# Layer 0's opening of a two-layer transformer on one core: first norm, modulation, keys, values and gates in a hand-written order

## The chip, the core and the metric

The kernel runs on one core of a Trainium2 chip. Its engines work in parallel, each in its own program order: TensorE (PE) multiplies matrices, VectorE (DVE), ScalarE (ACT) and GpSimd (POOL) do elementwise work, and SyncE (SP) issues the DMAs between HBM and SBUF. They meet through semaphores; an instruction that waits holds back everything behind it on its own engine. The metric is the device time of one execution in microseconds (us), lower is better. Before the change the median of three runs is 2780.57 us (2779.29 to 2788.6).

## The reference, cut to what matters

Two layers; the change touches only the beginning of layer 0: the modulated norm of 256 context and 1024 latent tokens, the projection to keys and values of the windowed attention, the 16 gates of the mLSTM, and the first queries.

```
mod_l = (silu(c) @ ada_w[0] + ada_b[0]).reshape(b, 1, 6, 1024)      # mod_c the same from c_ctx
h = rms_norm(x, norm1_g[0]) * (1 + mod[:, :, 1]) + mod[:, :, 0]     # for latents and for context
qa, ka, va, oa, ga, qb, kb, vb = split(h @ w_in)                    # 4 x 512, 16, 512, 128, 128 columns
g = (ga + gate_b) -> input gates and log_sigmoid(forget gates), forwards and backwards
qb, kb = rms_norm(qb, q_norm_g), rms_norm(kb, k_norm_g)             # per head of 64, then rope for latents
o_b = banded window attention(qb, kb, vb, context keys and values, sink)
h_a = mLSTM over chunks of 128, both directions (qa, ka, va, g)
y = concat(rms_norm(h_a) * sigmoid(oa), o_b) @ w_out;  x = x + mod[2] * y;  then the MLP;  then layer 1
```

## The kernel before, in words

Activations lie transposed: eight chunks of 128 channels (index j) on the partitions, tokens along the free axis. Tokens come in three groups, `TGS`: L1 (tokens 256 to 767) and L2 (768 to 1279) are latents, 512 columns each, and C (0 to 255) is the context. To multiply nearly in fp32 at the fast rate, each operand is split into a rounded part and a rest (`hhi`/`hlo` of the activations, `whi`/`wlo` of the weights), and each product takes three matmuls. A "unit" is one block of 128 output columns of a weight: 8 chunks x 3 matmuls for each group.

Layer 0 opens in `first` (in `body`). Modulation of shift and scale is made in four quarters (`ada_quarter`, L239): quarter q gives channels of chunks 2q and 2q+1 and needs 2 MB of `ada_w`, in four tiles s0f to s5f in rotation; eight 32-column matmuls (L254) on `cs`, the additions L259 and L261, four small matmuls with `asel2` (L264), and two DVE instructions that write `mod` and `gs`. The norm's sum of squares is taken by `norm_stats` (ACT squares, DVE and POOL add, one matmul with `ones`, L306) for L1 and L2, and by `sum_steps` for C. `norm_apply` makes, for each chunk, x * gs * rs on DVE (L375), `hhi` on ACT (L379), and `hlo` on DVE (L393) for even chunks or on ACT and POOL (L381, L390) for odd ones. The loop at the end of `first` multiplies each ready chunk with two units, the gates' (`U_G`, 16 columns in use out of 128) and the keys' (`U_KB`) at L2381.

Then `swa_setup` projects the values (weights in `mr` and `ir`, L423 to L425), transposes them (L1382), norms the keys (`qk_norm`), and `mixer0` makes the first queries, seven of the 48 steps of `gather` (the mLSTM's units, one group each) and `gates`. `swa` follows: 40 blocks of scores (first matmul L1457), softmax and values, with the remaining units, queries and modulation as fill between the blocks. `mlstm` comes behind it and needs what `gates` makes.

All this is written in Tile: a scheduler orders the instructions of each engine by its own estimates, and a tile's buffer is reused only when its last reader is done. Region reuse (`Area.place`, `Banks`) is by hand.

Of the kernel before, what the change touches and what calls it, by code (L numbers as in the profile page):

```python
# [19 lines left out]
P = 128  # L20
# [23 lines left out]
U_KB, U_VB, U_QB, U_G, U_M = 1, 2, 3, 0, 7  # L44
# [52 lines left out]
class Kernel:  # L97
# [141 lines left out]
    def ada_quarter(self, q, tp, psp):  # L239
# [4 lines left out]
        for kk in range(2):  # L244
            ps = psp.tile("D", "adaps")
            for e in range(2):
                w = tp.tile([P, 2, 2, 256], F32, tag="raw")
                k0 = 4 * kk + 2 * e
                src = a["ada_w"][0, k0 * P : (k0 + 2) * P, 0:2048].rearrange("(k p) (b n) -> p k b n", p=P, b=2)
                for b in range(2):  # L250
                    nc.sync.dma_start(w[:, :, b, :], src[:, :, b, q * 256 : q * 256 + 256])
                for i in range(2):
                    c = 2 * e + i
                    nc.tensor.matmul(  # L254
                        ps[32 * c : 32 * c + 32, :], self.cs[:, k0 + i, :], w[:, i, :, :].rearrange("p b n -> p (b n)"),
                        start=True, stop=True, tile_position=(0, 32 * c),
                    )
            if kk == 0:
                nc.scalar.activation(acc, ps, AF.Copy)  # L259
            else:  # L260
                nc.vector.tensor_tensor(acc, ps, acc, op=ALU.add)  # L261
        pt = psp.tile("D", "adapt")
# [13 lines left out]
        )  # L276

# [211 lines left out]
    def qk_norm(self, ps, t0, n, vv, tabs, g, hd, qscale, tp, ss):  # L489
# [5 lines left out]
        rs = self.qk_rms(n, st, hd, qscale, tp, ss)  # L495
# [698 lines left out]
    def gates(self, kp, cbt, psp, dr, gy):  # L1194

        nc = self.nc
        ta, tb = self.slot(2, F32), self.slot(3, F32R)
# [6 lines left out]
        for x in (mr, ir):  # L1204
            nc.gpsimd.memset(x.bitcast(F32), 0.0)
# [4 lines left out]
        gd = dr.tile([4, 4, T], F32, tag="gd", name="gd")  # L1210
        for i in range(4):
            nc.sync.dma_start(gd[i], gy[32 * i : 32 * i + 4, :])
# [82 lines left out]
    def mixer0(self, first):  # L1295
# [8 lines left out]
        with ExitStack() as ctx:  # L1304
            kp = self.pool(ctx, "kp", side="right")
            with ExitStack() as c2:
# [3 lines left out]
                gy, heads = first(wp, kp)  # L1310
                psp = self.banks(A=(0, 1), B=(2, 3), Q=(4,), S=(5,))
                tp = self.area(6 * PG, 8 * PG)
                self.qt_bufs = 1
                tr = tp.tile([P, 512], F32, tag="qsw")[:, : 2 * P].rearrange("p (d q) -> p d q", d=2)
                nc.sync.dma_start(tr, a["tri"].rearrange("d p q -> p d q"))
                nc.vector.tensor_copy(tri, tr)
# [11 lines left out]
                tb = self.area(5 * PG, 6 * PG)  # L1328
                psa = self.banks(A=(0, 1, 2), B=(7,), Q=(4,), G=(3, 5))
                st, qs = self.swa_setup(sp, tp, tb, psa, wp, heads, gy)  # L1330
                for _ in st[-1](psa, 0, qs):
                    pass
                self.gps = self.banks(A=(6, 7))
                heads = [self.gather(wp, tb, ud, h) for h in range(4)]
                for _ in range(7):
                    next(heads[0])
                mr, ir, cb, tq = self.gates(kp, small, psa, dr, gy)
                self.gps = psp
                self.swa(sp, small, tb, psp, wp, mixd, heads, st, qs)
# [22 lines left out]
    def swa_setup(self, sp, tp, tb, psp, wp, heads, gy):  # L1362

        nc, a = self.nc, self.a
        KH = [sp.tile([P, T], F32R, tag=f"s{v}", name=f"KH{v}") for v in range(2)]
        KL = [sp.tile([P, T], F32R, tag=f"s{2 + v}", name=f"KL{v}") for v in range(2)]
        VV = [sp.tile([P, NT // 2, 2, P], F32R, tag=f"s{4 + i}", name=f"VV{i}") for i in range(2)]
        tt = self.area(0, 2 * PG)
        tabs = self.rope_tables(tt, a["rope0"], V_SK, V_SKS, "r0")
        wp.place("raw", cuts(self.F, PG, 2 * PG))  # L1370
        wp.place("adaraw", cuts(self.F, PG, 3 * PG, 4 * PG))
        tb.tile([P, 512], F32, tag="ev")
        for t0, n, vv in TGS:
            s = slice(t0, t0 + n)
            ps, ks = heads[t0]
            nc.scalar.activation(gy[:, s], ps[:, :n], AF.Identity, bias=self.v(V_GB))
            ps = self.proj(psp, "A", heads["v"], t0, n)
            t = tb.tile([P, 512], F32, tag="adaacc", name="vt")
            nc.scalar.activation(t[:, :n], ps[:, :n], AF.Copy)
            pt = psp.tile("B", "vT")  # L1380
            for i in range(n // P):
                nc.tensor.transpose(pt[:, i * P : (i + 1) * P], t[:, i * P : (i + 1) * P], self.ident)  # L1382
            src = pt[:, :n].rearrange("p (c v d) -> p c v d", v=2, d=64)
            for i in range(2):
                c0, c1 = max(t0 // P, 5 * i), min((t0 + n) // P, 5 * i + 5)
                if c0 < c1:
                    for v in range(2):
                        o = VV[i][:, c0 - 5 * i : c1 - 5 * i, v, :]
                        self.split(o[:, :, 0:64], o[:, :, 64:128], src[:, c0 - t0 // P : c1 - t0 // P, v, :], nc.vector)
            t = self.qk_norm(ks, t0, n, vv, tabs, V_SK, 64, False, tp, psp.tile("Q"))  # L1390
# [8 lines left out]
        tabs = self.rope_tables(tt, a["rope0"], V_SQ, V_SQS, "r0")  # L1399

        def queries(psp, pr, qs):
            w = self.unit(wp, a["win0"][U_QB + pr])
            qs += [self.slot(2 * (pr % 2) + h, F32R) for h in range(2)]
            for t0, n, vv in TGS:
                ps = self.proj(psp, "A", w, t0, n)
                t = self.qk_norm(ps, t0, n, vv, tabs, V_SQ, 64, True, tp, psp.tile("Q"))
                s = slice(t0, t0 + n)
                for h in range(2):
                    src = t[64 * h : 64 * h + 64, :n]
                    own = qs[h][64 * h : 64 * h + 64, s]  # L1410
                    nc.scalar.activation(own, src, AF.Copy)
                    nc.gpsimd.tensor_tensor(
# [1016 lines left out]
```

## Time and profile before

| | |
|---|---|
| median of 3 runs | 2780.57 us |
| the profiled execution | 2788.63 us, its span 2786.8 us |
| PE busy in the span | 2695.9 us (97%) |
| DVE, ACT, POOL busy | 1885.0, 1476.7, 1095.2 us |
| mean granted clock of TensorE | 0.992 |

The page says that PE is the busiest engine at 97%; in its 40 slices only the first shows 6 of 10. A slice is 70 us long, so the opening has to be cut finer. Times in the rows are us from the span's start. Matmul records overlap their neighbours, so the pace of matmuls is read from the distance of their starts, not from their durations.

### The profile page before, as it was taken

Reading aid. Unit: us, or ns where it says so; the run is one execution under the profiler, and the core shown is the slowest. Engines: PE = TensorE matmul, PEld = TensorE weight load, DVE = VectorE, ACT = ScalarE, POOL = GpSimd, SP = SyncE. Lnnn points to the kernel's source line nnn. Section 1 sums busy time; section 2 is a strip of 40 time slices with the busy share of each in tenths; the row PEclk is TensorE's granted clock in tenths of the full one; section 3 lists DMA queues with packets and bytes.
Section 4 is the critical chain, followed back from the end, with each engine's and each line's share of the span. In section 5 each row is a group of like instructions: output and inputs, shape, how many; then the busy total and the mean of one; then the engine's idle time right before and its main releaser. Section 6 shows DMA issues by size and latency. Waiting matters only on the chain.

```text
span 2786.8 us, 40782 instructions
## 1 busy us (share of the span) xinstructions
PE 2695.9 (97%) x14683; PEld 2284.5 (82%) x14683; DVE 1885.0 (68%) x3268; ACT 1476.7 (53%) x2611; POOL 1095.2 (39%) x744
## 2 busy tenths in 40 slices
PE   6899999999999999999999999999999999999999
PEld 3688788878788888878878889999988888888877
DVE  4645655677876766557678757888874677666676
ACT  4654554445564444344436557888865554444432
POOL 3430220000237576530001346787865499740000
PEclk9999999999999999999999999999999999999999
DMA  7122233363335667488756710000045155577664
GB/s 241 56 84 100 79 104 112 108 210 99 110 108 174 209 220 237 157 307 286 246 166 218 243 61 26 24 28 20 26 150 195 65 174 192 175 284 263 215 223 154
DMA packets 194659, 428.33 MB, mean 154 GB/s; under 512 B 21128, under 2 KB 47336, under 8 KB 194456
## 3 DMA queue, kind: packets, MB, share of 16 engines
q1 hardware_dynamic: 194456, 425.73, 45.6%
q8 instruction: 115, 1.88, 0.3%
q14 instruction: 88, 0.72, 0.1%
HBM read 322.90 MB, written 102.74 MB: 153 GB/s over the span
## 4 chain that ended last, share of the span: by engine, by line
PE 73%; DVE 6%; DMA 4%; issue 3%; ACT 2%; POOL 1%; DVEq 0%; SPq 0%; POOLq 0%; ACTq 0%
PE psum L588 21%; PE psum L1046 17%; PE psum L423 4%; PE psum L2017 4%; PE psum L424 4%; PE psum L425 4%; PE psum L2203 3%; PE psum L1142 3%; PE psum L1924 3%; DMA hhiraw<-in_w 2%; DVE W L398 2%; POOL W L398 1%; PE psum L1500 1%; PE psum L2079 1%; PE psum L1506 1%
## 5 line engine op out<-in xcount | busy, mean ns | idle before, releaser
L398 POOL TENSOR_TENSOR W<-F,W 128x512 fp32r<-128x512 f32 (+2 forms) x319 | 489.1, 1547 | 519.4 <-ACT W L397 438.8
L1046 PE MATMUL psum<-W,W 128*128 128x512 f32 x2688 | 617.8, 391 | 10.9 <-DVE W L398 4.7
L1046 PEld LDWEIGHTS psum<-W,W 128*128 128x128 f32 x2688 | 504.6, 188 | 123.6 <-DVE W L398 10.9
L588 PE MATMUL psum<-hhi,W 128*128 128x512 f32 (+1 forms) x1600 | 442.2, 356 | 2.3 <-DVE x L1774 0.9
L397 ACT ACTIVATE W<-F 128x512 fp32r<-128x512 f32 (+2 forms) x380 | 275.1, 739 | 292.6 <-POOL F L561 99.4
L588 PEld LDWEIGHTS psum<-hhi,W 128*128 128x128 f32 x1600 | 285.1, 189 | 46.3 <-issue 2.5
L588 PE MATMUL psum<-hlo,W 128*128 128x512 f32 (+1 forms) x800 | 284.3, 355 | 0.0
L397 ACT ACTIVATE W<-hhiraw 128x1024 fp32r<-128x1024 f32 x98 | 104.0, 1061 | 316.2 <-PE psum L1046 235.4
L423 PE MATMUL psum<-hhi,W 128*128 128x512 f32 (+1 forms) x624 | 232.8, 373 | 0.9 <-ACT F L1432 0.9
L424 PE MATMUL psum<-hlo,W 128*128 128x512 f32 (+1 forms) x624 | 227.3, 364 | 0.0
L425 PE MATMUL psum<-hhi,W 128*128 128x512 f32 (+1 forms) x624 | 227.1, 364 | 0.0
L969 DVE TENSOR_TENSOR hhiraw<-hhiraw 128x512 f32<-128x512 f32 x154 | 108.3, 712 | 108.4 <-DMA hhiraw<-in_w 107.6
L561 POOL TENSOR_TENSOR F<-F 128x512 f32<-128x512 f32 x112 | 164.8, 1471 | 13.5 <-DMA F<-in_w 4.5
L588 PEld LDWEIGHTS psum<-hlo,W 128*128 128x128 f32 x800 | 151.2, 189 | 21.4 <-issue 0.2
L390 POOL TENSOR_TENSOR hlo<-F,hhi 128x512 fp32r<-128x512 f32 (+1 forms) x24 | 27.4, 1144 | 347.6 <-ACT F L381 347.6
L398 DVE TENSOR_TENSOR W<-hhiraw,W 128x1024 fp32r<-128x1024 f32 x98 | 119.6, 1221 | 60.7 <-ACT W L397 58.2
L423 PEld LDWEIGHTS psum<-hhi,W 128*128 128x128 f32 x624 | 118.4, 190 | 21.3 <-ACT x L397 2.5
L424 PEld LDWEIGHTS psum<-hlo,W 128*128 128x128 f32 x624 | 118.5, 190 | 17.3 <-issue 2.2
L425 PEld LDWEIGHTS psum<-hhi,W 128*128 128x128 f32 x624 | 118.3, 190 | 17.3 <-issue 0.5
L588 PE MATMUL psum<-x,W 128*128 128x512 f32 x504 | 123.5, 389 | 0.0
L398 DVE TENSOR_TENSOR W<-hloraw,W 128x1024 fp32r<-128x1024 f32 x98 | 119.4, 1218 | 0.7 <-ACT W L397 0.7
L2203 PE MATMUL psum<-W,W 128*128 128x512 f32 (+1 forms) x408 | 109.5, 372 | 2.4 <-POOL W L398 1.5
(450 smaller groups left out, 6231.2 us busy)
## 6 DMA issues: line engine op xcount, KB each, us to landing
F<-in_w SPq DMA_DIRECT2D x104, 512.0 KB
hloraw<-hd SPq DMA_DIRECT2D x90, 512.0 KB
hhiraw<-in_w SPq DMA_DIRECT2D x72, 512.0 KB
hd<-F SPq DMA_DIRECT2D x142, 256.0 KB
hhiraw<-in_w SPq DMA_DIRECT2D x116, 256.0 KB
F<-in_ada_w SPq DMA_DIRECT2D x96, 256.0 KB
hd<-x SPq DMA_DIRECT2D x90, 256.0 KB
F<-in_win SPq DMA_DIRECT2D x33, 512.0 KB
```

Source lines behind the costliest of these rows:

```text
L397: nc.scalar.activation(hi, src, AF.Copy)
L398: eng.tensor_tensor(lo, src, hi.bitcast(F32), op=ALU.subtract)
L423: nc.tensor.matmul(ps, sh, mh, start=i == 0, stop=False)
L424: nc.tensor.matmul(ps, sh, ml, start=False, stop=False)
L425: nc.tensor.matmul(ps, sl, mh, start=False, stop=i == n - 1)
L561: add = lambda o, p, q, how: nc.gpsimd.tensor_tensor(o, p, q, op=how)
L588: nc.tensor.matmul(ps, w[i][:, p], B[j][k], start=first and j == 0 and m == 0, stop=last and j == 3 and m == 2)
L969: tt = lambda o, p, q, how: eng.tensor_tensor(o, p, q, op=how)
L1046: nc.tensor.matmul(bank(base + i), A[u][:, p], B[v], start=first and m == 0, stop=last and m == 2)
L1142: nc.tensor.matmul(bank(k), B[u][:, i * P : i * P + P], A[v][:, half], start=f == 0 and m == 0, stop=f == NFF - 1 and m == 2,)
L2017: nc.tensor.matmul(u.o[:, :QT], v[x], p[y], start=c == 0 and m == 0, stop=c == 2 * NB - 1 and m == 2)
L2203: self.nc.tensor.matmul(ps, x[:, c], y, start=first and m == 0, stop=last and m == 2)
```

## The change: what it does

1. The opening is issued inside `manual_schedule`: on all engines the instructions stand in the order in which the code issues them, from the first load to the first queries and seven gather steps.
2. Group C is loaded first, then quarter 0, then the units of values and keys, L1, quarter 1, L2, quarters 2 and 3. `ada_quarter` becomes a generator with five steps (load, load, products, products, sums), so loads stand far ahead of the products.
3. Squares are summed by matmuls with `ones` (8 for C, 8 for L1, 4 for L2 after pairwise additions on DVE), not on DVE and POOL.
4. x is scaled by the norm in place for several chunks ahead (`scale`); when a quarter is there, `prepare` makes `hhi` on ACT and the rest on DVE, and POOL has no share in it.
5. Beside keys, the opening multiplies values and not gates. The gates' weight shrinks to 32 columns and is not split: `gate_rows` multiplies it in plain fp32 with `hhi` and `hlo`, the three groups at three column positions, after three gather steps.
6. The first mLSTM unit (`own`) takes the place in `mr` and `ir` that the values' had, and its steps stand between the steps of the key norm.
7. The elementwise part of the gates (`gates`) runs in the last of the four head pairs of `swa`, at its first block.

```diff
+        w0 = load(0)
+        yield
+        w1 = load(1)
+        yield
+        products(0, w0)
+        yield
+        products(1, w1)
+        yield
         pt = psp.tile("D", "adapt")
         for i in range(4):
             nc.tensor.matmul(pt[:, 2 * i : 2 * i + 2], acc[:, i * P : (i + 1) * P], self.asel2, start=True, stop=True)
...
+        def add_up(g, s, j, last=ND - 1):
...
+            nc.tensor.matmul(parts[g], k.ones, s, start=j == 0, stop=j == last)
...
+        def scale(g, js):
...
+            for j in js:
+                nc.vector.tensor_tensor(y, y, rs[g][:, :n], op=ALU.mult)
...
+        def prepare(g, j):
...
+            nc.scalar.activation(hi, y, AF.Identity, scale=gs, bias=sh)
+            if j % 2 and not vv:
+                nc.scalar.activation(h, y, AF.Identity, scale=gs, bias=sh)
+            else:
+                nc.vector.tensor_scalar(h, y, gs, sh, op0=ALU.mult, op1=ALU.add)
+            nc.vector.tensor_tensor(lo, h, hi.bitcast(F32), op=ALU.subtract)
...
+        both(C, 2, 3)
+        scale(L1, range(2, 4))
+        add_up(L2, two_squares(0), 0, 3)
+        both(L1, 2)
...
+        add_up(L2, two_squares(3), 3, 3)
+        rms(L2)
+        run(2)
+        run(3)
...
+        scale(L2, range(4))
+        both(L2, 0, 1)
+        run(2)
+        both(L2, 2)
+        run(2)
+        both(L2, 3)
+        scale(L2, range(4, 6))
+        both(C, 4)
+        both(L1, 4)
+        run(3)
+        both(L2, 4)
...
+        def gate_rows():
+            for j in range(ND):
+                for m, h in enumerate((self.hhi, self.hlo)):
+                    for q, t0, n, o in ps:
+                        nc.tensor.matmul(
+                            o, w[:, j, :], h[:, j, t0 : t0 + n].bitcast(F32),
+                            start=j == 0 and m == 0, stop=j == ND - 1 and m == 1, tile_position=(0, 32 * q),
+                        )
...
+                if (pr, blk) == (3, 0):
+                    g = gates()
```

SP issues the opening's loads. Before (x_118 is chunk 0 of x, s0f to s5f the tiles of a quarter, F the raw weights):

```order
L131 DMA x_125<-in_x 128x512
L414 DMA F<-in_win 128x1024 x3
L251 DMA s0f<-in_ada_w 128x2x256 x2
L251 DMA s1f<-in_ada_w 128x2x256 x2
L251 DMA s2f<-in_ada_w 128x2x256 x2
L251 DMA s3f<-in_ada_w 128x2x256 x2
L131 DMA x_118<-in_x 128x512
```

and now, with the eight loads of C ahead of it:

```order
L131 DMA x_125<-in_x 128x256
L252 DMA s0f<-in_ada_w 128x2x256 x2
L252 DMA s1f<-in_ada_w 128x2x256 x2
L252 DMA s2f<-in_ada_w 128x2x256 x2
L252 DMA s3f<-in_ada_w 128x2x256 x2
L2487 DMA F<-in_win 128x1024 x2
L131 DMA x_118<-in_x 128x512
```

Half as much of x stands ahead of quarter 0, and the three weight loads have become two behind it.

On DVE, quarter 2 read before (L261 adds a quarter's halves, L268 and L273 write `mod` and `gs`, L375 and L393 are `norm_apply`; x_118 to x_125 are chunks 0 to 7 of x):

```order
L261 TENSOR_TENSOR F<-psum,F 128x512
L268 TENSOR_TENSOR mod_82<-psum,vec 128x2x4
L273 SCALAR_TENSOR_TENSOR gs_169<-mod_82,vec 128x4
L375 SCALAR_TENSOR_TENSOR F<-x_122,gs_169,F 128x512
L375 SCALAR_TENSOR_TENSOR F<-x_123,gs_169,F 128x512
L375 SCALAR_TENSOR_TENSOR F<-x_122,gs_169,F 128x512
L393 SCALAR_TENSOR_TENSOR hlo<-F,mod_82,hhi 128x512
```

and the stretch around quarter 2 now (L2516 scales x, L2528 and L2529 are `prepare`, L268 adds the halves, L284 and L289 write `mod` and `gs`):

```order
L2516 TENSOR_TENSOR x_121<-x_121,F 128x512
L2528 TENSOR_SCALAR F<-x_118,gs_172,mod_82 128x512
L2529 TENSOR_TENSOR hlo<-F,hhi 128x512 x2
L268 TENSOR_TENSOR F<-psum,F 128x512
L2528 TENSOR_SCALAR F<-x_120,gs_172,mod_82 128x512
L2529 TENSOR_TENSOR hlo<-F,hhi 128x512
L284 TENSOR_TENSOR mod_82<-psum,vec 128x2x4
L289 SCALAR_TENSOR_TENSOR gs_172<-mod_82,vec 128x4
L2529 TENSOR_TENSOR hlo<-F,hhi 128x512
L2516 TENSOR_TENSOR x_122<-x_122,F 128x512
```

Each addition of a quarter now has `prepare` steps of other chunks behind it.

On PE, quarters 2 and 3 met before as follows (L254 are a quarter's products, L264 its small matmuls, L2381 a chunk's products with W_105, the gates', and W_106, the keys'):

```order
L254 MATMUL psum<-s4f,cs 32x512 x2
L254 MATMUL psum<-s5f,cs 32x512 x2
L264 MATMUL psum<-asel_64,F 128x2 x4
L254 MATMUL psum<-s0f,cs 32x512 x2
L254 MATMUL psum<-s1f,cs 32x512 x2
L2381 MATMUL psum<-hhi,W_105 128x512
L2381 MATMUL psum<-hhi,W_106 128x512
```

and the stretch around quarter 2 now (L2504 sums squares, L261 are a quarter's products, L2539 the chunks' products with W_105, now the values', and W_106, the keys'):

```order
L2504 MATMUL psum<-F,ones 128x512 x2
L261 MATMUL psum<-s2f,cs 32x512 x2
L261 MATMUL psum<-s3f,cs 32x512 x2
L2539 MATMUL psum<-hhi,W_105 128x512 x2
L2539 MATMUL psum<-hlo,W_105 128x512
L2539 MATMUL psum<-hhi,W_106 128x512 x2
L2539 MATMUL psum<-hlo,W_106 128x512
```

A quarter's products come in two separate halves, with the products of one or two chunks between.

## Rows read from the trace of the kernel before

**Rows 1.** Stretches: length, busy of PE, PEld, DVE, ACT, POOL (instructions), clock, DMA, GB/s

```profile
0.00:15.00 15.00, 0.01 (x1) 0.01 (x1) 7.64 (x44) 7.74 (x12) 3.44 (x8) 1.00 0.82 278
15.00:27.00 12.00, 7.96 (x26) 2.24 (x26) 2.43 (x5) 5.43 (x8) 8.04 (x4) 0.98 1.07 366
27.00:40.00 13.00, 10.15 (x31) 4.72 (x32) 6.96 (x10) 7.44 (x14) 2.56 (x2) 0.76 0.91 284
40.00:72.00 32.00, 26.67 (x116) 16.84 (x115) 14.64 (x28) 11.72 (x20) 7.05 (x5) 0.88 0.45 141
72.00:92.38 20.38, 19.38 (x92) 15.50 (x93) 12.62 (x27) 15.46 (x33) 7.76 (x9) 0.86 0.12 31
92.38:166.30 73.92, 64.47 (x321) 51.93 (x320) 32.45 (x55) 39.28 (x75) 33.70 (x22) 1.00 0.23 79
166.30:558.00 391.70, 385.94 (x2319) 320.59 (x2318) 226.99 (x775) 205.51 (x467) 64.35 (x39) 0.99 0.29 98
```

**Rows 2.** Waits of PE in the first 300 us: total, times, longest

```profile
PE psum L306 <- DVE F L321: 15.0, 1, 15.0
PE psum L2381 <- ACT hhi L379: 7.2, 5, 2.1
```

**Rows 3.** Waits of DVE from 15 to 92 us

```profile
DVE F L261 <- PE psum L254: 18.9, 3, 8.7
```

**Rows 4.** PE's timeline, 22 to 62 us: start, length, [idle before it]

```profile
22.20 1.05 PE L254 MATMUL psum<-s3f,cs 128*32 128x512 f32 x4 [0.45 <-DMA s3f<-in_ada_w]
24.10 1.05 PE L264 MATMUL psum<-asel,F 128*128 128x2 f32 x8 [0.85 <-DVE F L261]
27.15 1.22 PE L2381 MATMUL psum<-hhi,W 128*128 128x512 f32 x2 [2.00 <-ACT hhi L379]
...
53.43 0.62 PE L254 MATMUL psum<-s2f,cs 128*32 128x512 f32 x1
53.43 0.62 PE L254 MATMUL psum<-s3f,cs 128*32 128x512 f32 x2
53.45 0.62 PE L254 MATMUL psum<-s4f,cs 128*32 128x512 f32 x1
```

**Rows 5.** PE's timeline, 72 to 95 us, and the first scores

```profile
72.31 1.22 PE L2381 MATMUL psum<-hhi,W 128*128 128x512 f32 x2 [2.06 <-ACT hhi L379]
...
76.69 0.63 PE L2381 MATMUL psum<-hhi,W 128*128 128x512 f32 x1
77.12 0.63 PE L2381 MATMUL psum<-hlo,W 128*128 128x512 f32 x1
...
92.38 0.40 PE L423 MATMUL psum<-hhi,mrv 128*128 128x512 f32 x1
...
93.54 0.40 PE L425 MATMUL psum<-hhi,irv 128*128 128x512 f32 x1
93.78 1.02 PE L494 MATMUL psum<-F,blk 128*128 128x512 f32 x2
94.64 0.65 PE L1382 MATMUL psum<-ident,F 128*128 128x128 f32 x4
...
166.34 0.36 PE L1457 MATMUL psum<-KH,x 128*128 128x256 f32 x1
```

**Rows 6.** Groups of equal shape, 0 to 175 us: busy, mean ns | idle before

```profile
L379 ACT ACTIVATE hhi<-F,mod 128x512 fp32r<-128x512 f32 x16 | 11.1, 719 | 14.7 <-DVE F L375 14.6
...
L379 ACT ACTIVATE hhi<-F,mod 128x256 fp32r<-128x256 f32 x8 | 3.7, 500 | 1.6 <-DVE F L375 1.6
...
L499 DVE TENSOR_TENSOR F<-F 128x512 f32<-128x512 f32 x4 | 2.8, 693 | 2.7 <-POOL F L470 2.7
```

**Rows 7.** Groups of 27 to 95 us

```profile
L450 DVE TENSOR_SCALAR F<-F,vec 128x1024 f32<-128x1024 f32 x1 | 0.7, 744 | 0.0
```

**Rows 8.** Waits of PE from 166 to 558 us

```profile
PE psum L1506 <- ACT x L397: 2.0, 4, 0.9
PE psum L1507 <- DVE ptl L398: 1.7, 1, 1.7
```

## What the change does to the time, predicted before it ran

> **What bounds the kernel now.** I read the busy table by stretches first. From 166.3 us, the first scores, to 558 us PE is busy 385.9 of 391.7 us: there PE itself is the bound, and whatever reaches the first scores earlier is kept. In the opening it is not: busy 0.01 of the first 15 us, 7.96 of 12, 10.15 of 13, 26.67 of 32, 19.38 of 20.4 up to 92.38 us, where the last chunk product stands, and 64.47 of 73.92 behind it [rows 1]. That is 28 us without a matmul ahead of 92.38 us and 9.4 us behind, and part of the busy time is slow: the granted clock is 0.76, 0.88 and 0.86 in three stretches, between the two levels of 1.2 and 2.4 GHz.
>
> Then the waits. PE waited 15.0 us once, for the sum of squares of the first latents, and 7.2 us in five waits for ACT's hhi [rows 2]. DVE waited 18.9 us for the products of the quarters [rows 3]. So the opening is a chain: load, quarter, gs, chunk, product. PE's rows show the price of a wait: after 2.06 us of idling, matmuls of 512 columns start 0.43 us apart (76.69, 77.12), where otherwise they start 0.24 apart (93.54, 93.78) [rows 5], half the clock.
>
> The later instructions keep their order: in the listing the last two thirds of PE's rows are the same, and the number of gather steps ahead of the first scores is seven in both. So the forecast is the new time of the first scores, against 166.34 us [rows 5], and what the gates cost later.
>
> **The work that is moved, in PE time.** Prices: 0.232 us for a matmul of 512 columns, half of it for 256; an fp32 matmul with 512 columns 0.86 (93.78 to 94.64) [rows 5]. A latent chunk with two units is six matmuls, 1.4 us, a context chunk 0.7. The gates' unit leaves the opening (48 x 0.232 + 24 x 0.116 = 13.9 us) and the values' unit moves in: nothing changes there. Added are 20 sums of squares, 8 x 0.43 + 12 x 0.86 = 13.8 us, where three had been: about 11.5 us more for PE, taken from DVE and POOL, in a stretch where PE idles 28 us. I cost them by what waits behind them, below.
>
> The gates come back as 16 sets of three 32-column fp32 matmuls. Four such matmuls of a quarter stand at 53.43 to 53.45 us together, two from s3f and one each from s2f and s4f [rows 4]; a lone matmul of this width would need 0.86, so a set should take about 0.9 us, and 16 sets 14.4 us. That is what the old unit took. In turn, a set would be 0.86 + 0.43 + 0.86 = 2.15 and all 34.4; I keep that as a rival.
>
> **When the last chunk product ends.** I step through the new order with durations of the rows: a DVE pass over 512 columns 0.69, one with a single operand 0.37 (half of 0.744 for 1024), an ACT pass 0.72, or 0.50 for 256 [rows 6, 7]; a quarter's half 0.9 and its small matmuls 1.05 [rows 4].
>
> First, arrival. 278 GB/s for 15 us and 366 GB/s behind it [rows 1]: C (1.05 MB), quarter 0 (2.1), two units (1.05) and L1 (2.1) are 6.3 MB, of which 4.17 have moved by 15 us and the rest by 20.8. Before, s3f was byte 5.8 MB, moved at 19.4 by the same count, and its product began at 22.20 [rows 4]: 2.8 us of lag. So L1 is there at 23.6 us. Its sums of squares end between 25.1 (one square and one matmul behind the load) and 31.2 us (all eight matmuls behind it, 6.9 us); as the first context chunks stand ahead of them on PE, I take 30.0.
>
> From there, leg by leg. Two ACT passes, one scale, one hhi: 2.7, first latent product at 32.7. PE then has chunk, half quarter, chunk, small matmuls (4.75), and the context chunks 2 and 3 wait 0.9 for mod, gs and hhi, to 38.4; DVE has 1.1 for their rests (256 columns, half the price), two scales and one addition of squares behind that: first sum for L2 at 41.5. Now DVE sets the pace, nine passes of 0.69 and one of 0.37, with 0.5 for ACT between: 48.6, last sum done 49.5. L2's norm 1.3, four scales and the first rest, 5.1 in all: 54.6. Products, half quarter, then DVE's addition, which waits for that half with the next rest behind it, products, small matmuls, mod, and another rest: 62.6 for chunk 3 of L2. DVE for scales and chunk 4 3.1, PE 1.8, ACT's copy and hhi 1.3, a rest, then 3.9 of products and the second half of quarter 3: 73.4. Again the addition, two scales and a rest on DVE (2.8), four matmuls and small matmuls (2.0), mod and hhi: 79.0. Six last chunks are 7 us for PE and 6.4 for ACT with a rest and four matmuls behind: **87.0 us**, against 92.4.
>
> Two things are left out there, with opposite signs. Waits near 2 us stand at about 32, 50 and 53 us, and after such a wait PE was at half clock for 5 us (72.31 to 77.12) [rows 5]: 3 to 4 us more. And passes that follow each other start closer than their duration, which takes some 3 us from DVE's legs. I keep 87, bounds 84 and 91.
>
> **Behind it.** To the first scores, PE has 168 matmuls of 512 (own, queries, four more gather steps; 39.0 us), 72 of 256 (8.4), ones for the head norms (4.3), ten transposes (1.0) and the gates (14.4): 67.1. Before, this took 73.9 with 64.5 busy [rows 1]. In the new order the steps of own stand between transposes and head sums, so that ACT's copies and DVE's chain have 5.6 us of matmuls beside them, and weights for the queries come 10 us before they are due. I allow 1.5 us of waits (bounds 0 and 9.4, as before). 87.0 + 67.1 + 1.5 = 155.6, 10.7 us before 166.3.
>
> **The gates later.** Some forty DVE instructions and seven ACT ones join the last head pair. DVE is busy 227 of 391.7 us there and PE's largest waits in this stage are 2.0 and 1.7 us in total [rows 1, 8]. One us, bounds 0 and 4. The loads of the gates' tables and the round trip through DRAM have ten blocks of time, about 95 us, as 391.7 us hold 40 blocks and the rest.
>
> Sum: -10.7 + 1 = -9.7 us. The profiled execution took 2788.63 us, span 2786.8, and would become 2778.9; that execution lies at the upper end of the runs, so I subtract from the median, 2780.57: **2770.9 us**.
>
> **The rivals.**
> Fewer waits: PE alone would need 37.7 us from 32.7 on, to 70.4. If half of the waits that I stepped through fall away, the end is at 79 and the gain 18 us: 2763. For it: the order was laid out chunk by chunk, quarters are loaded by 44 us (14.7 MB). Against: DVE alone has, counted in the listing, some 35 us of passes there.
> More waits: the chain quarter, addition, rest is as long as I have it, half clock comes on top (91), and the gates take 4 us from the softmax: -3.7, 2777. For it: DVE waited 18.9 us for quarters before [rows 3], and the order still has every addition ahead of other chunks' rests.
> The three gate matmuls of a set stand in turn: + 20 us, to 2791. Against it are the rows at 53.43. The Trainium skill says so too ("TensorEngine Tiling (Array Packing)", Key Properties: tiles of the array load weights and multiply in parallel).
> Half clock throughout: if short bursts between waits never bring the fast clock, the 37.7 us become 75.4, the end is at 108, 21 us later than forecast, and the kernel takes 2792, slower. Place and price are the stretch from 32.7 us; it decides from about half of that, as 10 us more eat the gain. Against: before, with 5 waits for hhi, the clock was 0.76 to 0.88, not 0.5. The Trainium skill speaks for it: "TensorE: Matmul & The Clock Gate", section What's actually happening, has the slow clock as the default and activity as what lifts it. By that alone the sum would be 2792; the row's clock is nearer to the fast level, so its chance is small.
> That the order isn't kept is no rival: the listing shows each engine's rows as the code issues them.
>
> **How the numbers follow.** 0.3% is 8.3 us, about what a measurement can tell from no change. The forecast's own range, 84 to 91 for the end and 0 to 4 for waits and gates, is 2767 to 2776, chance 0.48; it lies on the bound, so 0.26 faster, 0.22 same. Fewer waits 0.22, faster. More waits 0.18, same. Gates in turn 0.06 and half clock 0.06, slower. Faster 0.48, same 0.40, slower 0.12. The range reaches from beyond the first rival, 2758, to 2785, where the two slow cases (0.12) and some of the faster tail are left out.
>
> **What would show it.** Right: sums of squares of L1 end near 30 us; the last chunk product 84 to 91; DVE's waits behind the products of quarters 2 and 3; a set of gate matmuls every 0.9 us; first scores near 156 us, and from there to the mLSTM the same 391 us. Wrong: DVE never idle between 50 and 80 us (then it is the bound, not the chain), sets 2.1 us apart, a clock near 0.5 between 33 and 80 us, scores blocks of the last pair longer than those before.

## The result and the profile after

The changed kernel takes 2794.61 us (median of 6 runs, 2790.32 to 2800.55) beside 2781.57 us for the kernel before (6 runs). The ratio is 1.0041, 95% interval 1.0024 to 1.0057: 0.4% slower, 13.0 us, where 9.7 us of gain were forecast. The forecast's direction and its range were wrong.

The profiled execution has a span of 2796.3 us against 2786.8, so the traces can explain 9.5 us of the 13.0; the one of the kernel before was the slowest of its runs (2788.6). The busy table by stretches, cut at the places that answer to [rows 1] (us; then busy time and number of instructions of PE, PEld, DVE, ACT and POOL; granted clock; DMA share; GB/s):

```profile
0.00:15.00 15.00, 9.30 (x28) 5.47 (x28) 4.28 (x39) 6.28 (x13) 0.52 (x5) 1.00 0.76 232
15.00:27.00 12.00, 7.80 (x31) 4.98 (x28) 7.81 (x16) 5.99 (x10) 2.44 (x1) 0.76 1.06 377
27.00:40.00 13.00, 10.71 (x36) 3.76 (x34) 3.14 (x5) 5.75 (x9) 0.00 (x0) 0.89 1.06 360
40.00:72.00 32.00, 24.18 (x96) 14.73 (x93) 18.15 (x35) 14.96 (x24) 0.00 (x0) 0.87 0.36 122
72.00:100.39 28.39, 23.23 (x100) 16.69 (x99) 16.34 (x29) 12.21 (x20) 2.56 (x1) 0.82 0.00 1
100.39:172.10 71.71, 68.35 (x360) 48.81 (x358) 28.45 (x43) 41.20 (x73) 29.61 (x20) 0.98 0.26 85
172.10:558.00 385.90, 376.95 (x2261) 312.55 (x2259) 229.34 (x772) 203.24 (x462) 67.13 (x43) 0.99 0.29 97
```

The last chunk product ends at 100.39 us (forecast 87.0; before 92.38), the first scores stand at 172.10 (forecast 155.6; before 166.34). From the first to the last scores it takes 385.0 us, before 381.1. From there to the end both take 2239 us. So 5.8 us are lost up to the first scores and 3.9 in the attention stage, and that is the difference of the spans. (Behind the last scores all kernels here do the same work, and it took 2233.5 to 2241.9 us in their traces: a difference of a few us between two whole spans says little about the opening.)

Two things are to be seen in the table. DMA is done early: 0.36 of a share from 40 to 72 us and nothing behind it. And DVE and ACT are busy for half of the time from 40 us on, so neither is full. PE is held up, and its clock is low in every stretch from 15 to 100 us. PE's waits from 33.4 to 100.5 us (who waited <- for whom: us in all, times, longest):

```profile
PE psum L2539 <- ACT hhi L2524: 7.6, 5, 2.0
PE psum L2539 <- DVE hlo L2529: 6.3, 6, 2.0
PE psum L2504 <- DVE F L2592: 1.3, 2, 1.2
```

That is 15.2 us in 13 waits. What follows a wait shows in PE's timeline (start, us, operation, count, and in brackets the idle time before it):

```profile
82.82 0.60 PE L261 MATMUL psum<-s3f,cs 128*32 128x512 f32 x2
83.35 0.73 PE L2539 MATMUL psum<-hhi,W 128*128 128x512 f32 x2
86.06 0.79 PE L2539 MATMUL psum<-hlo,W 128*128 128x512 f32 x1 [1.98 <-DVE hlo L2529]
86.65 1.05 PE L2539 MATMUL psum<-hhi,W 128*128 128x512 f32 x2
87.51 0.63 PE L2539 MATMUL psum<-hlo,W 128*128 128x512 f32 x1
87.93 1.70 PE L280 MATMUL psum<-asel,F 128*128 128x2 f32 x8
90.72 0.79 PE L2539 MATMUL psum<-hhi,W 128*128 128x256 f32 x2 [1.09 <-ACT hhi L2524]
```

The second half of quarter 3 stands at 82.8 (forecast: ends 73.4). DVE adds it first and makes the next chunk's rest after that, and PE waits 1.98 us. The products then stand 0.43 us apart (86.65 to 87.51 for two), the small matmuls take 1.70 us, where [rows 4] had 1.05, and the next wait comes before the clock is back. From the first latent product, 36.48, to the end are 63.9 us. 13.2 of them are waits, so 50.7 are left for work that was priced at 37.7. Not all of these 13 us are half clock. The granted clock was at its lower level in four stretches (columns as in the busy table):

```profile
38.20:41.70 3.50, 3.50 (x13) 1.08 (x12) 1.05 (x2) 0.00 (x0) 0.00 (x0) 0.51 0.59 188
45.10:48.50 3.40, 3.24 (x12) 2.71 (x12) 3.19 (x7) 2.98 (x7) 0.00 (x0) 0.50 0.11 36
62.10:65.50 3.40, 3.40 (x12) 2.12 (x14) 0.00 (x0) 0.44 (x1) 0.00 (x0) 0.50 1.00 378
86.00:96.30 10.30, 9.15 (x31) 7.90 (x31) 6.09 (x11) 6.23 (x10) 2.56 (x1) 0.50 0.00 0
```

PE was busy for 19.3 us in them, with work that takes half as long at full clock: half clock cost 9.6 us. The other 3.4 are work that took 41.1 us at full clock and was priced at 37.7. Part of it is the restart: the first product behind a wait stands 0.34 us ahead of the next one (61.28, 61.62), where 0.23 is usual.

Behind the chunk products one wait stands out, and half clock after it (the starts from 113.54 on are 0.43 apart):

```profile
112.65 0.50 PE L440 MATMUL psum<-hhi,mrv 128*128 128x512 f32 x1 [3.36 <-DVE x L501]
113.54 0.63 PE L440 MATMUL psum<-hhi,mrv 128*128 128x512 f32 x1
113.97 0.63 PE L441 MATMUL psum<-hlo,mrv 128*128 128x512 f32 x1
117.09 0.40 PE L440 MATMUL psum<-hhi,mrv 128*128 128x512 f32 x1
```

Own's second step needs PSUM bank 7, where the context's key sums lie until the key norm (L501) has read them, and ACT's part of that norm stands behind eight copies for L1 and L2.

The gates' matmuls go in sets of three, every 0.86 us, as [rows 4] let expect (13.9 us for all):

```profile
124.55 0.59 PE L1453 MATMUL psum<-hhi,x 128*32 128x512 f32 x1
124.56 0.40 PE L1453 MATMUL psum<-hlo,x 128*32 128x256 f32 x1
124.57 0.59 PE L1453 MATMUL psum<-hhi,x 128*32 128x512 f32 x1
...
125.41 0.59 PE L1453 MATMUL psum<-hlo,x 128*32 128x512 f32 x1
```

In the attention stage every block of scores stands 5.2 us later than before, up to 418.8 us. There 2.15 us are added at once. DVE's timeline and POOL's at that place, and at the one where the rest is lost:

```profile
422.28 2.43 DVE L1604 TENSOR_SCALAR small<-small 128x2 f32<-128x2 f32 x1
422.42 2.29 DVE L415 TENSOR_TENSOR ptl<-psum,x 128x512 fp32r<-128x512 f32 x1
...
469.99 2.40 DVE L1284 TENSOR_TENSOR x<-x 128x128 f32<-128x128 f32 x1
```

```profile
422.42 1.17 POOL L1227 MEMSET mr<- 128x1280 f32 x1
423.52 1.16 POOL L1227 MEMSET ir<- 128x1280 f32 x1
...
469.88 2.37 POOL L415 TENSOR_TENSOR W<-F,W 128x1024 fp32r<-128x1024 f32 x1 [12.91 <-ACT W L414]
```

An instruction of DVE on 128x2 elements (0.16 elsewhere) took 2.43 us: it ended when POOL's two memsets, which `gates` now issues here, were done. PE waited 1.28 and 0.42 us behind it. At 470 us a pass of the gates (L1284) took 2.40 us beside POOL's weight split, and PE's wait behind it, up to 474.25 us, was 2.92 us, against 1.57 before.

### The profile page after: what moved, and what is told of

Read it like the earlier page. It is cut to its first block, busy times and chain, and to the rows that moved or that the text cites. A ratio compares the mean times of both kernels' runs of the same rounds, so it can differ in the third digit from the quotient of the medians.

```text
span 2796.3 us, 40888 instructions
## 1 busy us (share of the span) xinstructions
PE 2712.1 (97%) x14741; PEld 2287.5 (82%) x14741; DVE 1888.7 (68%) x3284; ACT 1475.2 (53%) x2606; POOL 1068.9 (38%) x726
## 4 chain that ended last, share of the span: by engine, by line
PE 77%; DVE 8%; DMA 5%; ACT 4%; issue 3%; POOL 2%; SPq 0%; DVEq 0%; POOLq 0%; ACTq 0%
PE psum L610 21%; PE psum L1068 15%; PE psum L440 5%; PE psum L442 5%; PE psum L441 5%; PE psum L2149 4%; PE psum L2335 3%; PE psum L1164 3%; DMA hhiraw<-in_w 3%; PE psum L2056 3%; DVE W L415 2%; POOL W L415 1%; PE psum L1629 1%; PE psum L2539 1%; PE psum L1635 1%
## 5 line engine op out<-in xcount | busy, mean ns | idle before, releaser
L610 PE MATMUL psum<-hhi,W 128*128 128x512 f32 (+1 forms) x1600 | 442.2, 356 | 2.8 <-DVE x L665 1.1
L610 PEld LDWEIGHTS psum<-hhi,W 128*128 128x128 f32 x1600 | 285.0, 189 | 46.9 <-issue 1.6
L610 PE MATMUL psum<-hlo,W 128*128 128x512 f32 (+1 forms) x800 | 284.3, 355 | 0.0
L440 PE MATMUL psum<-hhi,W 128*128 128x512 f32 (+1 forms) x600 | 224.6, 374 | 0.0
L442 PE MATMUL psum<-hhi,W 128*128 128x512 f32 (+1 forms) x600 | 218.3, 364 | 0.0
L441 PE MATMUL psum<-hlo,W 128*128 128x512 f32 (+1 forms) x600 | 218.0, 363 | 0.0
L440 PEld LDWEIGHTS psum<-hhi,W 128*128 128x128 f32 x600 | 113.8, 190 | 20.6 <-issue 2.8
L407 POOL TENSOR_TENSOR hlo<-F,hhi 128x256 fp32r<-128x256 f32 (+1 forms) x12 | 13.1, 1091 | 305.8 <-ACT F L398 305.1
L442 PEld LDWEIGHTS psum<-hhi,W 128*128 128x128 f32 x600 | 113.5, 189 | 16.1 <-issue 0.2
L2056 PE MATMUL psum<-hhi,W 128*128 128x256 f32 x512 | 111.1, 292 | 0.3 <-DVE F L1969 0.3
```

What stands on the lines that cost most here:

```text
L440: nc.tensor.matmul(ps, sh, mh, start=i == 0, stop=False)
L441: nc.tensor.matmul(ps, sh, ml, start=False, stop=False)
L442: nc.tensor.matmul(ps, sl, mh, start=False, stop=i == n - 1)
L610: nc.tensor.matmul(ps, w[i][:, p], B[j][k], start=first and j == 0 and m == 0, stop=last and j == 3 and m == 2)
L2056: nc.tensor.matmul(ps, s[:, c], m[:, j, t0 : t0 + QT], start=j == 0 and i == 0, stop=j == ND - 1 and i == 2)
```

## The experiments

Theory A: PE loses in the opening to half clock behind its many short waits. Rival B: DVE's and ACT's passes set the pace. Theory C: the order itself makes the waits, as it leaves quarters 2 and 3 late. All ratios are to the kernel before.

### e1: extra matmuls in the waits

```diff
+        def fill(n):
+            for _ in range(n):
+                nc.tensor.matmul(k.psum[:, o : o + P], k.ident, k.ones, start=True, stop=True)
...
+        fill(9)
         multiply(L1, 0)
```

> The changed kernel with 63 extra fp32 matmuls of 128 columns on TensorE (0.21 us each at full clock, 13 us in all; their results are not used) set into ten of the waits of the opening, between 33.4 and 100.4 us; nothing else differs. Theory A (half of the 14 us lost there is a consequence: each wait of 1 to 2 us is followed by several us of matmuls at half clock): with PE kept busy in the waits the products run 0.23 apart, the last chunk product ends at 87 to 92 instead of 100.4, the granted clock between 40 and 92 us is above 0.95, and the kernel takes 2782 to 2787, 8 to 12 less than the changed kernel. Rival B (the passes of DVE and ACT set the pace, the half clock only fills time in which PE would wait): the waits grow by what the clock gives, the last chunk product stays at 97 or later, the time at 2791 to 2798.

Measured: 1.0027 (1.0016 to 1.0038), 2788.2 us; last chunk product done at 95.3 us, first scores 168.25. Neither range was met. The table by stretches:

```profile
40.00:72.00 32.00, 30.04 (x172) 22.23 (x172) 20.98 (x40) 15.04 (x24) 0.00 (x0) 1.00 0.37 123
72.00:95.32 23.32, 21.85 (x128) 16.29 (x128) 13.50 (x23) 12.03 (x19) 2.54 (x1) 1.00 0.00 1
```

The clock is at its upper level throughout. But 63 x 0.23 = 14.6 us of extra matmuls (nine took 2.09) and 3.4 us of waits that are left come to 18 us, more than the 15.2 in whose place they stand. So of the 9.6 us that half clock had cost about 5 came back. Most of the others went into these longer waits, filled or not. The intervals of e1 and of the changed kernel overlap, so the 5 us rest on the trace alone.

### e2: another order

```diff
-        run(1)
-        run(2)
-        scale(L1, range(2))
-        prepare(L1, 0)
...
+        scale(L1, range(2, 4))
+        run(2)
+        run(3)
+        multiply(C, 2)
+        multiply(C, 3)
+        prepare(L1, 2)
+        s = two_squares()
+        prepare(L1, 3)
+        run(2)
+        multiply(L1, 2)
+        run(2)
...
+        for j in range(0, ND, 2):
+            scale(L2, range(j, j + 2))
+            both(L2, j, j + 1)
```

> The changed kernel with another order between the sums of squares of L1 and the last chunk product, same instructions: both halves of quarters 2 and 3 and their small matmuls come as soon as their loads can be there (all modulation done near 52 us instead of 88), the rests of the next chunks stand ahead of the additions that wait for a half, and chunks 0 to 7 of L2 come last. If the waits come from the order (quarters 2 and 3 late, DVE held behind additions): last chunk product at 78 to 86 us instead of 100.4, waits of PE there under 7 us in all instead of 15, first scores at 150 to 158, 2773 to 2782 in all. Rival: DVE's 35 us of passes or ACT's 31 set the pace whatever the order: last product at 95 or later, DVE idle under 5 us between 34 us and it, 2788 or more.

Measured: 0.9998 (0.9989 to 1.0007), 2780.1 us, 0.43% under the changed kernel (from the two ratios); last chunk product done at 85.6, first scores 157.23. All but the waits as expected, and these are nearly so; from 33 to 86 us:

```profile
PE psum L2539 <- DVE hlo L2529: 4.4, 6, 2.5
PE psum L2539 <- ACT hhi L2524: 2.4, 3, 1.2
PE psum L280 <- DVE F L268: 1.0, 1, 1.0
```

7.8 us in place of 15.2, with the same instructions on the same engines. Half clock fell as much: the lower level was granted only from 80.4 us on, with 4.4 us of busy PE up to the last product, so it cost 2.2 us and not 9.6:

```profile
80.44:85.58 5.14, 4.44 (x11) 3.37 (x12) 2.67 (x4) 1.97 (x5) 0.00 (x0) 0.50 0.00 0
```

Theory C holds, and B falls as what set the pace of the changed kernel: 15 us of the opening were order, half of them waits and half the slow clock behind these, as A has it. One wait of 2.46 us is left late, and DVE's timeline and POOL's show what it is:

```profile
76.36 3.47 DVE L2516 TENSOR_TENSOR x<-x,F 128x512 f32<-128x512 f32 x2
```

```profile
76.75 2.54 POOL L415 TENSOR_TENSOR irv<-F,mrv 128x1024 fp32r<-128x1024 f32 x1 [55.77 <-ACT mrv L414]
```

Two passes that take 1.29 together took 3.47, beside POOL's split of own's weight.

### e3: memsets to DVE

```diff
-            self.tc.keep_in_program_order(nc.gpsimd.memset(x.bitcast(F32), 0.0))
+            nc.vector.memset(x.bitcast(F32), 0.0)
...
-        nc.vector.tensor_tensor(row, row, self.ident, op=ALU.mult)
+        nc.gpsimd.tensor_tensor(row, row, self.ident, op=ALU.mult)
```

> The changed kernel with two kinds of instruction of the gates moved between engines: the two memsets of mr and ir (128x1280) from POOL to DVE, and one 128x128 product (row times identity) from DVE to POOL. If the 2.4 us that a 128x2 instruction of DVE took beside the memsets, and the 2.4 us that the 128x128 product took beside POOL's weight split, come from DVE waiting for POOL, then from the first to the last scores it takes 381 to 382.5 us instead of 385.0 (before the change 381.1), and the kernel 2790 to 2792. Rival: the forty added instructions of DVE cost it, wherever the memsets run: 384 or more, no change in the time.

Measured: 1.0028 (1.0018 to 1.0038), 2788.1 us. DVE's timeline at the same place:

```profile
416.73 0.22 DVE L1604 TENSOR_SCALAR small<-small 128x2 f32<-128x2 f32 x1
416.87 0.68 DVE L415 TENSOR_TENSOR ptl<-psum,x 128x512 fp32r<-128x512 f32 x1
```

The stall is gone, and from the next block on (430 us) the scores stand 2.25 us earlier, counted from the first ones, than in the changed kernel: the price of the memsets, which covers what was lost there. The second edit tested nothing: the pass that stood was L1284, the input gates less b, not the product that I moved (L1280), and it stood again for 2.40 us. The stage as a whole took 383.75 us, not 381 to 382.5: behind the wait of 2.92 us, which is the same 2.9 in the changed kernel, e1, e2, e3 and e4, the stretch up to the next blocks varied between executions by 4.5 us (3.3 less in e1, 1.15 more in e4). By the granted clock, half clock behind that wait lasted 6.8 us in the changed kernel, none in e1, 3.4 in e2 and 10.2 in e3 and e4.

This run shows more. Its opening is that of the changed kernel, instruction for instruction, with nearly the same waits (7.6, 6.6 and 2.3 us), and yet its first latent product came at 35.16, not 36.48, and its last chunk product was done at 96.5, not 100.4:

```profile
40.00:72.00 32.00, 22.58 (x98) 14.06 (x97) 19.58 (x38) 15.05 (x24) 0.00 (x0) 0.95 0.35 121
72.00:96.50 24.50, 19.32 (x94) 13.49 (x93) 14.60 (x25) 12.03 (x19) 2.55 (x1) 0.93 0.00 1
```

The clock is 0.95 and 0.93 where it was 0.87 and 0.82. Worked out as above, half clock cost 4.9 us from the first latent product on, not 9.6. So how much of it nearly the same waits bring differs from execution to execution, by 4 us at the end of the opening, and e1's 5 us are little more than that.

### e4: the context's key norm earlier

```diff
         k_first(L1)
+        k_rms(C)
         v_split(L1)
         v_copy(L2)
         k_first(L2)
-        k_rms(C)
```

> The changed kernel with the context's key norm (k_rms of C) issued ahead of the splits of the values of L1 and of L2's first steps, not behind them. If the wait of 3.36 us at 112.65 is only ACT's order in front of bank 7: the wait goes, the half clock behind it too, first scores at 166 to 169 instead of 172.1, the kernel 3 to 6 us faster than the changed kernel (2788 to 2792). Rival: the next wait in the chain (key sums of L1, splits) takes its place: first scores at 171 or later, no change in the time.

Measured: 1.0032 (1.002 to 1.0044), 2789.5 us. The wait of 3.36 us is gone, another came up, 1.9 us for the copy of L2's values (L1402). From the last chunk product to the first scores it took 69.8 us, 1.9 less than 71.7. The first scores stand at 169.76, between what was expected and the rival's. That the time lies in the expected range shows little: its interval and the changed kernel's overlap.

### e5: e2 with own's rest on DVE

```diff
-            if j == 4:
-                weights_split(own, nc.gpsimd)
+        weights_split(own, nc.vector)
```

> The kernel of e2 (other order) with one more edit: the rest of own's weight (128x1024) is made by DVE behind the last chunk's rest, not by POOL in the middle of L2's chunks. In e2 two passes of DVE at 76.36 us took 3.47 instead of 1.29 us beside POOL's 2.4 us on that weight, and PE then waited 2.46 us at 81.14 and ran at half clock to the last product. If DVE waits for POOL there: the pair of passes takes 1.3, the wait is under 0.5, the last chunk product ends at 80.5 to 82 instead of 85.4, first scores at 152 to 154.5, 2775 to 2778 in all. Rival (own's weight, now later and on DVE, holds up own's first product or the splits of the values): first scores at 156 or later, the time that of e2 (2780).

Measured: 0.9985 (0.9977 to 0.9994), 2776.0 us. The pair of passes takes 1.29 again, and PE's wait there is 0.27 us. The last product came at 84.1 and the first scores at 156.44, against what I expected: in the profiled execution PE was at half clock from 39.1 to 42.5 and from 49.3 to 52.7 us, where e2's was not (0.91 against 1.00 from 40 to 72 us). The median fell by the 4 us that were expected, the one trace shows 0.8 of them.

### e6: L1's squares in pairs

```diff
+            s, t = next(sq), next(sq)
+            nc.vector.tensor_tensor(s, s, t, op=ALU.add)
+            add_up(L1, s, i, 3)
```

> The changed kernel with L1's squares added in pairs on DVE, so that four fp32 matmuls sum them and not eight (as the change has it for L2). If the eight matmuls on the path are what makes L1's sums end at 33.4 instead of the forecast 30.0: they end at 28.5 to 30.5, the first latent product comes at 31.5 to 33.5 instead of 36.48, and the end moves with it by 3 to 4 us (the clock's share of it varies by as much between executions). Rival: the loads of quarter 1 or the squares on ACT hold what follows: first latent product at 35 or later.

Measured: 1.0044 (1.0032 to 1.0056), 2792.2 us; first latent product at 36.09. A miss. PE's timeline (an fp32 matmul counts as two):

```profile
26.72 4.88 PE L2504 MATMUL psum<-F,ones 128*128 128x512 f32 x6 [1.40 <-DVE F L2578]
31.95 1.13 PE L2504 MATMUL psum<-F,ones 128*128 128x512 f32 x2 [0.35 <-DVE F L2578]
33.01 0.62 PE L261 MATMUL psum<-s4f,cs 128*32 128x512 f32 x2
```

Three sums take 4.88 us, 1.63 each in place of 0.86, and ACT's sixth square stood 4.12 us for a buffer that the first of them still read. Half the matmuls at half the clock end when all of them did.

### e7: all parts

It is e2, e4, e5, e6, the memsets of e3, and this:

```diff
-            for o, (_, wh, wl) in zip(heads[t0], w):
-                for m, (x, y) in enumerate(((wh, hi), (wl, hi), (wh, lo))):
+            for m in range(3):
+                for o, (_, wh, wl) in zip(heads[t0], w):
+                    x, y = ((wh, hi), (wl, hi), (wh, lo))[m]
```

> All that the runs point to in one kernel: the order of e2, own's rest on DVE as in e5, pairs as in e6, the context's key norm early as in e4, the two memsets on DVE as in e3, and in each chunk the four products with hhi ahead of the two with hlo. If the parts are separate: last chunk product at 75 to 79 us, first scores at 143 to 149, 381 to 384 from there to the last scores, 2761 to 2769, faster than both kernels. Rival: once PE is fed, DVE's 35 us of passes become the bound and the parts overlap: last product at 81 or later, first scores at 151 or later, 2772 or more.

Measured: 0.9982 (0.9974 to 0.999), 2776.0 us; last product done at 82.4, first scores 153.60. The rival's numbers: from 62 us on, DVE's passes for a pair of L2's chunks need 3.15 of 3.59 us, and for the other 0.44 DVE waits for ACT. Once PE is fed, DVE is nearly full.

### e8: L1's squares added on DVE

```diff
+        for t in sq:
+            nc.vector.tensor_tensor(r, acc, t, op=ALU.add)
+            acc = r
+        add_up(L1, r, 0, 0)
         scale(C, range(2, ND))
```

> The changed kernel with L1's eight squares added one by one on DVE as they come (seven passes of 0.69 us), ahead of the scaling of C's chunks 2 to 7, so that one fp32 matmul sums them and no buffer of ACT's squares waits for PE. In e6, with four matmuls, ACT stood 4.1 us for PE and the four ran at half clock, so L1's sums ended as late as with eight. If that is what held e6: the sum ends at 28 to 30 us, the first latent product starts at 31 to 33.5 instead of 36.48 and everything up to the first scores comes 3 to 5 us earlier, 2787 to 2791 in all (the clock's share varies by 4 us between executions). Rival: the quarters' loads or the order behind set the end, and the first scores stay at 170 to 173.

Measured: 1.0033 (1.0021 to 1.0045), 2791.1 us; first scores 168.68. PE's timeline:

```profile
29.11 2.08 PE L2504 MATMUL psum<-F,ones 128*128 128x512 f32 x2 [4.58 <-DVE F L2578]
31.11 1.06 PE L261 MATMUL psum<-s4f,cs 128*32 128x512 f32 x2
34.49 1.22 PE L2539 MATMUL psum<-hhi,W 128*128 128x512 f32 x2 [1.44 <-ACT hhi L2524]
```

The sum is done at 31.1 us, 2.3 earlier than the eight, but this one matmul takes 2 us, and quarter 1 and the first chunk go on at half clock. 6 us of PE work were saved, and the first latent product gained 2.0. Both came later than expected, and the 3.4 us by which the first scores are earlier are within what the clock alone varies (e3).

### e9 and e10: a better order, and matmuls to keep the clock

e9 is e7 with the sum of e8, without the order of products in a chunk, and:

```diff
+        run(1)
+        run(2)
+        add_up(L1, r, 0, 0)
...
+        v_copy(L2)
         k_first(L1)
         k_rms(C)
...
+            if j < 6:
+                scale(L2, range(j + 2, j + 4))
             both(L2, j, j + 1)
```

> The order of e2 with own's rest on DVE (e5), L1's squares added on DVE as in e8 with quarter 1's first half ahead of the sum, the scalings of L1's and L2's last chunks one pair ahead of their use, the copy of L2's values and the context's key norm early on ACT (e4), and the two memsets on DVE (e3). In e7 PE and DVE took 3.59 us for each pair of L2's chunks, of which DVE waited 0.44 and PE had 2.8 to do, L1's first product came at 35.9, and a wait of 3.0 us for the copy of L2's values stood behind the last chunk. If these three are separate: first latent product at 31 to 33, pairs 3.2 us apart, last chunk product at 75 to 78.5 instead of 82, first scores at 143 to 148 instead of 153.6, 2765 to 2771 in all, less than e7's 2776. Rival: quarter 1's loads (there near 29 us) and DVE's passes hold the middle, the last product stays at 80 or later, 2774 or more.

Measured: 0.9958 (0.9945 to 0.9972), 2771.4 us, faster than both kernels. On DVE the pairs stand 3.05 us apart, nearly as expected, but the first latent product came at 35.43, the last was done at 83.25, and the first scores stand at 153.10, 0.5 before e7's. Of the 5.7 us between the two profiled spans, 2.1 lie up to the last scores and the others behind, where the two do the same work. So that e9 beats the kernel before is measured; why it beats e7 is not settled. e10 adds 17 of e1's matmuls between 25 and 35 us.

> The kernel of e9 with 17 extra fp32 matmuls of 128 columns (results not used), 4 and 7 around quarter 1's first half and 6 ahead of the first latent product, where PE waits between 25.4 and 35.4 us. In e8 and e9 the granted clock is 0.55 to 0.63 between 27 and 40 us, 0.89 in the changed kernel, whose eight fp32 sums kept PE busy there. If the time that the fewer sums saved was given back as half clock: with PE busy the products from 35 to 46 us run 0.23 apart, the second latent chunk is done by 40 instead of 42.9, last chunk product at 80 to 81.5 instead of 83.2, 2767 to 2770. Rival: the extra matmuls themselves run at half clock (0.43 each, 7 us in all) and push L1's sum or first product back to 36 or later: no gain, 2771 to 2775.

Measured: 0.9956 (0.9939 to 0.9973), 2770.5 us; last product done at 80.6, first scores 150.42. The clock from 27 to 40 us of e9, and below it of e10:

```profile
27.00:40.00 13.00, 10.04 (x31) 3.76 (x27) 8.21 (x16) 4.14 (x6) 0.00 (x0) 0.63 1.07 364
```

```profile
27.00:40.00 13.00, 11.64 (x66) 7.53 (x65) 9.70 (x22) 5.24 (x8) 0.00 (x0) 0.89 1.08 364
```

Work that nobody needs brought the last chunk product 2.7 us forward in the trace, as expected, though half clock stood there too, from 38.1 to 41.5 us. In the medians it is 1 us, which the intervals do not tell from nothing.

## Why the prediction was wrong, step by step

**The sums of L1, 30.0 forecast, 33.4 found, outside the bounds.** The eight matmuls started at 24.9, behind the context chunks, and took 8.57 us, not 6.9, at half clock until 28.0 us (0.82 on the whole). The context chunks were late themselves: `gs` of quarter 0 took DVE 1.54 us beside POOL's split of the values' weight. The leg behind them, given as 2.7, makes 2.85 by its own prices and took 3.1. e6 and e8 show that fewer matmuls there do not buy that time back one for one.

**The legs, 54.3 us from the first latent product to the end (32.7 to 87.0), 63.9 found.** This is the step that failed. The term that was wrong in it is half clock: 3 to 4 us more, set off against 3 us less for passes that follow each other closely, net 0. It cost 9.6 us, which is the whole overrun. The rest of the leg's sum came out at 54.3 by luck: waits were 13.2 us, not 16.6, and work 41.1, not 37.7. I had taken the price of one wait from [rows 5] and applied it to three waits near 2 us, where there were 12 behind the first latent product, several only 2 to 5 us apart, and many a next one fell into the last one's slow stretch. The size could have been read from [rows 1]: clocks of 0.76, 0.88 and 0.86 over 13, 32 and 20.4 us are up to 9.8 us lost already in the kernel before. Whether the 3 us off were there no run shows; DVE did idle (4.6 and 2.5 us for the quarters, as the "what would show it" had it), and two prices of the legs were too low: a pass with a single operand took 0.54 us, not 0.37, and ACT's copies 0.80, not 0.72. Taking half clock away gave back 5.4 of the 9.6: in e1 58.5 us were still needed from the first latent product on, 15.9 of them waits and extra matmuls.

**The order.** The steps took the order as given and asked only what its legs cost. e2 shows what that left out: same instructions, 15 us less. The last loads of quarter 3 went out at 57 us, as their tile was free only when quarter 2's first half was multiplied at 56, and three additions stood ahead of other chunks' rests.

**Behind the chunk products, 68.6 forecast, 71.7 found.** The work was right (67.1), the sets of gates too. The 1.5 us of waits were 3.36, for a bank that I had not followed, with 3.4 us of half clock behind it, 1.7 us lost; e4 got 1.9 of them back. The cover that I named for own's steps (5.6 us of matmuls) was short by ACT's eight copies.

**The gates in the last head pair, +1 (0 to 4) forecast, +3.9 found.** Within the bounds, with another mechanism, so by luck. I counted instructions of DVE; 2.25 us are two memsets of POOL, which hold DVE up (e3). Most of the others come with the longer wait that ends at 474 us, where the clock alone makes 4.5 us between executions; their cause is not shown.

**The rivals.** Gates in turn fell (0.86 us a set). Fewer waits fell. Half clock throughout had the right size (2792) and the right place, and I gave it 0.06. The size is luck: it put the end of the legs at 108, which came at 100.4, and the rest was lost behind them. The clock was at its lower level not throughout but for 20.5 of 63.9 us. It was the right mechanism with the wrong condition: not "never fast", but slow again behind some of the waits, in four stretches for 12 waits. More waits, with half clock "on top", had the signs right and kept a gain only since it took the end at 91. (Its own terms, 91 and 4 us, make -2.7 and not -3.7: 2778. And the bound of 9.4 us for the waits behind the chunk products is not in the forecast's own range.)

## What to carry to other kernels

Price a wait of TensorE with the stretch behind it, and count the waits that fall into one another's stretch: here 13.2 us of waits brought 9.6 us of half clock with them. Before pricing a hand-written order, ask for each load and each producer how early it could run: an instruction that waits (an addition for a half quarter) should stand behind all work of its engine that doesn't. When work moves to POOL, look at what DVE does beside it.

## What the runs showed of the hardware

- POOL holds DVE up in whole instructions. Four places: 2.43 us for a 128x2 pass beside two memsets, 2.40 for 128x128 and 3.47 in place of 1.29 beside weight splits, and `gs` of quarter 0 at 1.54. A pass of DVE that reads PSUM ran at its usual 0.69 at 421.7 us, beside POOL's split of 420.08 to 422.48. The Trainium skill ("SBUF — State Buffer", Who interferes with whom) says that a DVE instruction with two inputs in SBUF contends with a GpSimd instruction that reads SBUF, not with one that only writes it, and that one in a 2-port mode, which a tensor_scalar can enter, contends with GpSimd, where whoever issues first blocks the other for the whole instruction. The four places agree with it: the three beside splits have two inputs in SBUF, and the one beside the memsets was a tensor_scalar; in which mode it ran no trace shows.
- The clock behind a wait is not the same from run to run. The same instructions with nearly the same waits ended at 96.5 and at 100.4 us, and the stretch behind one wait of 2.9 us varied by 4.5, with none to 10.2 us of half clock in it.
- Fewer matmuls in front of a chain can be worth little: eight fp32 sums took 8.57 us, one took 2.08 in a stretch with a clock of 0.55.
